# A hybrid-mixer layer on one core: meta tokens in the first attention tile, scans for running sums, per-tile bank drains, an earlier residual fetch and a rearranged end

## The chip, the cores and the metric

One core of one Trainium2 chip runs the whole layer in one launch. The metric is the device time of that launch in microseconds (us); lower is better. TensorE does the products, VectorE (DVE) and ScalarE (ACT) the element-wise work, GpSimd (POOL) a little of it and some transfers, SyncE (SP) issues most transfers.

## The reference, cut to what matters

16 meta tokens stand ahead of 256 tokens of width 2048. The layer is an RMS norm, one wide projection, four mixers of 512 columns each (an SSD state-space mixer, a windowed pooling mixer, FOX attention with a forget bias, and DSA attention whose keys are picked by an index score), an output projection, a residual, and a gated FFN of width 5632 with a short causal convolution on the gate. All in float32; only the last 256 rows are returned.

```python
h = rms_norm(x, g_mix_pre);  u = h @ w_in                      # 272 x 2048 @ 2048 x 4608 (padded)
y_a = ssd(silu(causal_dwconv(xbc)), dt=softplus(..), a=cumsum(dt * -exp(a_log)))
y_b = pool(u_pool);  y_c = fox(q, k, v, cumsum(log_sigmoid(f)));  y_d = dsa(q, c_kv, top 64 keys)
mix = concat(y_a, y_b, y_c, y_d) @ w_out;  x = x + rms_norm(mix, g_mix_post)
h = rms_norm(x, g_ffn_pre)
y = (silu(causal_dwconv(h @ w_gate)) * (h @ w_up)) @ w_down
return (x + rms_norm(y, g_ffn_post))[16:]
```

In FOX the score of a query i and a key j gets the bias F_i - F_j, F being the running sum of log_sigmoid; a softmax over j does not change if F_i is left out.

## The kernel before, in words

Each weight is split into two float32r parts (`split_hi` on ACT, L169, gives `whi`; `split_lo` on DVE, L175, gives `wlo`), and each product is taken three times (L230 to L232: hi*hi, hi*lo, lo*hi). The weights come in tiles of 1 MB, 184 of them in one `queue`; `load` (L134) issues them on SP two tiles ahead into three `raw` buffers, and the parts of the next tile are made while the present one is multiplied.

The projection runs in nine groups of 512 columns (`ORDER`: idx, dq, fk, fq, xs, fv, bc, z, pool), four weight tiles each. A group accumulates four blocks f = 0..3 of 128 columns in four PSUM banks (`acc`, four buffers). In a group's last tile `tile_matmuls` finishes f = 0, 1 in its first half and f = 2, 3 in its second. Then `scale` (L409) multiplies each bank by the row norm on DVE and so drains it; the next group's first product into a bank waits for that.

The mixers are Python generators (`small_values`, `dsa`, `fox`, `ssd`, `pool`). After each half of a weight tile `step(2)` advances the first two of them that are not held back by data, so that their small products lie between the large ones. `drain(name)` runs one to its end when the output projection needs it (order dsa, fox, ssd, pool). Each engine then works in order; its order is chosen by a planner that goes by what should be ready, except for operations under `pin` and in the manual stretch at the start of the FFN.

- `small_values` (L442) makes dt, the decays and their running sums: seven products with a triangular matrix (L485 to L491), transpositions (L500, L501), a row copy `drow` in DRAM, and four selections (L510 to L513).
- `attention` (L550) handles 128 queries at a time (qt = 1, 2): scores (L562, L565), row maximum (L570), eight exponentials (L573), division (L577), a copy of the meta weights (`sm`, L579), transpositions, and one output bank (L601, L606). The two last meta tokens' queries come after that, on their own (L614 to L645).
- `fox` rewrites its biases with sixteen DVE operations (L838, L843). `conv_silu` does the first term of the convolution on DVE (L726), the other three on DVE too (L728), then a Silu on ACT.
- In the first FFN group (two gate tiles, two up tiles, then the other four) `ffn_stats` fetches the tokens as rows into the room of `mo` (L1038, POOL's queue), adds them on DVE (L1047) and makes the second norm.
- The down projection accumulates eight banks (`po`); the last four of its 44 weight tiles are done for token block b = 0 and then for b = 1, each tile through all four banks. Then each block is squared on ACT, weighted on DVE (L1161), normed (L274 to L280) and added to the residual on DVE (L1175), with its transfers alternating between SP and ACT.

Of the kernel before, what the change touches and what calls it, by code (L numbers as in the profile page):

```python
# [1 line left out]

# [19 lines left out]
H = 8  # L22
# [5 lines left out]
OUT_CUTS = ((0, 256), (256, 256), (512, 512), (1024, 512), (1536, 512))  # L28
# [6 lines left out]
FIRST_CUTS = (0, 544, 1072, 1584, 2368, 3152)  # L35
# [19 lines left out]
NCOL = C_OWN + 8  # L55
# [33 lines left out]
def hybrid_layer(ctx: ExitStack, tc, t):  # L89
# [44 lines left out]
    def load(i):  # L134
# [3 lines left out]
        if i:  # L138
            raws[i] = wpool.tile([P, 2048], F32, tag="raw", bufs=3, name="raw")
        else:  # L140
            for q, (c0, c1) in enumerate(zip(FIRST_CUTS, FIRST_CUTS[1:])):
                (nc.scalar if q == 1 else nc.sync).dma_start(packed(c0, c1 - c0), t["first"][:, c0:c1])
            return
# [12 lines left out]
    def split_hi(i, half, n, pool=None):  # L156
# [6 lines left out]
        cuts = [1024 * q // n for q in range(n + 1)] if (i, half) != (0, 0) else [0, 256, 512, 1024]  # L163
# [43 lines left out]
    def tile_matmuls(accs, hi_lo, kts, n, feat, first, last, both=None, skip={}):  # L207
# [45 lines left out]
    def rstd_columns(small, sq, scale, segs, ps, meanwhile=None):  # L253

        n_seg, ng = len(segs), len(sq)
        order = [(g, j, i) for g in range(ng) for j in range(len(sq[g])) for i in (1, 2, 0)]
        for g, j, i in order:
            c0, n = segs[i]
            mm(ps[0:n, g * n_seg + i:g * n_seg + i + 1], sq[g][j][:, c0:c0 + n], ones[:, 0:1],
               start=(g, j, i) == order[0], stop=(j == len(sq[g]) - 1), skip_group_check=True)  # L260
# [24 lines left out]
    def rstd_rows(small, sq, scale, segs, out_rows):  # L285

        y = rstd_columns(small, sq, scale, segs, mix_ps())
        yield
        for g in range(len(sq)):
# [4 lines left out]
            act(out_rows[g], ps2[:, 0:tot], AF.Copy)  # L294

# [43 lines left out]
    G.dma_start(rows, bass.AP(tensor=t["rows"].tensor, offset=t["rows"].offset, ap=[[0, P], [1, 32]]))  # L339
# [53 lines left out]
    def project(g):  # L393
# [6 lines left out]
        for c in range(4):  # L400
            tile_matmuls(accs, lambda k: (xh[:, k, o:L], xl[:, k, o:L]), list(range(4 * c, 4 * c + 4)), n,
                         True, c == 0, c == 3, skip=SKIP.get(g, {}))
            if state["next"] == 4:
                nc.sync.dma_start(cols, t["cols"])
            if state["next"] == 7:
                load_small()
        return accs, n, o

    def scale(g, accs, n, o):  # L409
# [12 lines left out]
        else:  # L422
            u = q4(w=n, name=f"u{g}")
            for f in range(4):
                s = SKIP.get(g, {}).get(f, 0)
                V.tensor_tensor(u[:, f, s:], accs[f][:, s:n], rstd[:, o + s:L], ALU.mult)
                if g == G_Z:
                    act(u[:, f, :], u[:, f, :], AF.Silu)
            U[g] = u
        done.add(g)  # L430

# [10 lines left out]
    def small_values():  # L442
# [41 lines left out]
        pv = ps[:, 0:48].rearrange("p (s c) -> p s c", c=16)  # L484
        mm(pv[0:16, 0, :], upper[0:16, 0:16], val[0:16, 0, :], start=True, stop=True)  # L485
        mm(pv[:, 1, :], ones[0:16, :], val[0:16, 0, :], start=True, stop=False)
        mm(pv[:, 1, :], upper, val[:, 1, :], start=False, stop=True)
        mm(pv[:, 2, :], ones[0:16, :], val[0:16, 0, :], start=True, stop=False)
        mm(pv[:, 2, :], ones, val[:, 1, :], start=False, stop=False)
        mm(pv[:, 2, :], upper, val[:, 2, :], start=False, stop=True)  # L490
        mm(ps[:, 48:56], upper, val[:, 2, 0:8], start=True, stop=True)  # L491
        cum = M.tile([P, 56], F32, tag="cum", name="cum")
        V.memset(cum, 0.0)
        V.tensor_copy(cum[0:16, 0:16], ps[0:16, 0:16])
        V.tensor_copy(cum[:, 16:56], ps[:, 16:56])
        tok["cum"] = cum
        yield
        ps = mix_ps()
        for i, (c0, n) in enumerate(SEG):
            nc.tensor.transpose(ps[0:16, c0:c0 + n], cum[0:n, 16 * i:16 * i + 16], ident[0:n, 0:n])  # L500
        nc.tensor.transpose(ps[0:8, L:L + P], cum[:, 48:56], ident)  # L501
        rsb = M.tile([16, 400], F32, tag="rsb", name="rsb")
        V.memset(rsb, 0.0)
        act(rsb[:, 0:L], ps[0:16, 0:L], AF.Copy)
        act(rsb[0:8, L:400], ps[0:8, L:400], AF.Copy)
        G.dma_start(drow, rsb)
        done.add("rows")
# [3 lines left out]
        mm(ps[:, 16:24], sel_tok, cum[0:16, 0:8], start=True, stop=True)  # L511
        mm(ps[:, 24:32], sel_tok, dtv[0:16, 0, 0:8], start=True, stop=True)
        mm(ps[:, 64:64 + LQ], sel_ssd, rsb[:, L - LQ:L], start=True, stop=True)  # L513
        b0 = M.tile([P, 19], F32, tag="fb0", name="fb0")
        V.tensor_tensor(b0[:, 17:19], ps[:, 14:16], cols[:, C_PARITY:C_PARITY + 2], ALU.mult)
        V.tensor_tensor(b0[:, 16:17], b0[:, 17:18], b0[:, 18:19], ALU.add)
        V.tensor_scalar(b0[:, 0:16], ps[:, 0:16], -1.0, b0[:, 16:17], op0=ALU.mult, op1=ALU.add)
        V.tensor_tensor(b0[:, 15:16], b0[:, 15:16], col(C_MASK15), ALU.add)
# [31 lines left out]
    def attention(name, q, k, v, blk, bias):  # L550

        mh, ml = mixed_out(name)
        for qt, nk in ((1, 144), (2, 272)):
# [3 lines left out]
            for h0 in range(0, H, 2 * nb):  # L557
# [6 lines left out]
                for e, ps in enumerate(pair):  # L564
                    V.scalar_tensor_tensor(s[:, h0 + e:h0 + 2 * nb:2, :],  # L565
                                           ps[:, 0:nb * nk].rearrange("p (a b) -> p a b", b=nk), 0.125,
                                           bias_of(h0 + e, nb), op0=ALU.mult, op1=ALU.add)
# [63 lines left out]
        for _ in range(3):  # L631
            yield
# [613 lines left out]
```

## Time and profile before

| what | value |
|---|---|
| median of 3 runs | 1143.44 us (1143.44 to 1143.46) |
| profiled execution | 1145.26 us, of which the span of the trace is 1143.50 us |
| TensorE busy | 1127.9 us of the span, 7621 instructions |
| VectorE, ScalarE busy | 729.0 us, 556.7 us |
| transfers | 208.31 MB, mean 182 GB/s |
| granted TensorE clock, mean | 0.997 |

The busy time of TensorE counts an instruction until its result is written, and instructions overlap; the time between two starts is what one costs. A wait is put down to the instruction that ended it.

### The profile page before, as it was taken

The numbers are of one execution on the slowest core, as the hardware profiler recorded it, in microseconds if no ns is written. First come the engines' busy times: TensorE is split into PE (matmuls) and PEld (weight loads), VectorE is DVE, ScalarE is ACT, GpSimd is POOL, SyncE is SP. The second block draws the span as 40 slices with busy tenths as digits, with TensorE's granted clock in tenths as the row PEclk, the third lists the DMA queues.
The fourth block names the chain that finished last, engine by engine and source line by source line (L and its number), as shares of the span: only waits on it lengthen the run. The fifth ranks groups of instructions, "written<-read, shape, count | busy, mean of one in ns | idle before, by whom it ended". The sixth has DMA issues, their size and how long they took to land.

```text
span 1143.5 us, 18578 instructions
## 1 busy us (share of the span) xinstructions
PE 1127.9 (99%) x7621; PEld 1028.2 (90%) x7621; DVE 729.0 (64%) x1197; ACT 556.7 (49%) x811; POOL 30.1 (3%) x46
## 2 busy tenths in 40 slices
PE   9999999999999999999999999999999999999996
PEld 9999999988999989999899999998999888888885
DVE  7676595787655978656666576566565644555564
ACT  7334463674444756444544454445444444444452
POOL 0000021000000400000000000000000000000000
PEclk9999999999999999999999999999999999999999
DMA  8644435335455284555555555555555555555552
GB/s 319 246 161 175 150 130 185 130 122 196 157 191 184 88 323 180 177 193 185 184 185 185 185 184 185 184 185 185 184 186 185 191 188 191 193 193 184 184 184 74
DMA packets 32182, 208.31 MB, mean 182 GB/s; under 512 B 3521, under 2 KB 4193, under 8 KB 8801
## 3 DMA queue, kind: packets, MB, share of 16 engines
q1 hardware_dynamic: 29664, 197.49, 48.2%
q0 software_dynamic: 1712, 8.58, 2.3%
q8 instruction: 59, 0.97, 0.3%
q10 hardware_dynamic: 720, 1.06, 0.3%
q14 instruction: 27, 0.21, 0.1%
HBM read 204.99 MB, written 2.12 MB: 181 GB/s over the span
## 4 chain that ended last, share of the span: by engine, by line
PE 92%; DVE 5%; ACT 1%; issue 1%; DMA 1%; SPq 0%; DVEq 0%; ACTq 0%
PE acc L230 14%; PE mx L225 14%; PE acc L232 14%; PE acc L231 14%; PE mx L226 7%; PE acc L1131 4%; PE acc L1133 4%; PE acc L1132 4%; PE mx L1133 4%; PE mx L1131 4%; PE mx L1132 4%; DVE wlo L175 1%; PE mx L230 1%; PE mx L231 1%; PE mx L232 1%
## 5 line engine op out<-in xcount | busy, mean ns | idle before, releaser
L175 DVE TENSOR_TENSOR wlo<-raw,whi 128x1024 fp32r<-128x1024 f32 x369 | 447.8, 1218 | 324.3 <-ACT whi L169 322.7
L169 ACT ACTIVATE whi<-raw 128x1024 fp32r<-128x1024 f32 x369 | 385.0, 1051 | 460.0 <-PE acc L231 194.6
L225 PE MATMUL mx<-hx,whi 128*128 128x512 f32 x704 | 249.0, 396 | 0.0
L232 PE MATMUL acc<-hx,wlo 128*128 128x258 f32 x704 | 198.9, 283 | 1.0 <-DVE wlo L175 1.0
L226 PE MATMUL mx<-hx,wlo 128*128 128x256 f32 x704 | 198.2, 282 | 0.9 <-DVE wlo L175 0.9
L231 PE MATMUL acc<-hx,whi 128*128 128x258 f32 x704 | 198.9, 283 | 0.0
L230 PE MATMUL acc<-hx,whi 128*128 128x258 f32 x704 | 198.3, 283 | 0.0
L225 PEld LDWEIGHTS mx<-hx,whi 128*128 128x128 f32 x704 | 132.6, 188 | 31.1
L230 PE MATMUL acc<-xh,whi 128*128 128x272 f32 (+3 forms) x512 | 151.7, 298 | 1.4 <-DVE st L571 1.0
L231 PE MATMUL acc<-xl,whi 128*128 128x272 f32 (+3 forms) x512 | 146.1, 286 | 0.3 <-DVE xl L353 0.3
L232 PE MATMUL acc<-xh,wlo 128*128 128x272 f32 (+3 forms) x512 | 145.0, 287 | 0.0
L226 PEld LDWEIGHTS mx<-hx,wlo 128*128 128x128 f32 x704 | 133.1, 189 | 1.2 <-DVE wlo L175 1.2
L232 PEld LDWEIGHTS acc<-hx,wlo 128*128 128x128 f32 x704 | 132.9, 189 | 1.2 <-DVE wlo L175 1.2
L231 PEld LDWEIGHTS acc<-hx,whi 128*128 128x128 f32 x704 | 133.4, 189 | 0.3 <-DVE hx L1010 0.2
L230 PEld LDWEIGHTS acc<-hx,whi 128*128 128x128 f32 x704 | 132.4, 189 | 0.6
L230 PEld LDWEIGHTS acc<-xh,whi 128*128 128x128 f32 x512 | 96.5, 189 | 8.2 <-issue 5.2
L231 PEld LDWEIGHTS acc<-xl,whi 128*128 128x128 f32 x512 | 96.7, 189 | 1.3 <-issue 0.7
L232 PEld LDWEIGHTS acc<-xh,wlo 128*128 128x128 f32 x512 | 95.7, 188 | 0.6 <-issue 0.3
L1132 PE MATMUL acc<-whi,yl 128*128 128x512 f32 x176 | 69.6, 395 | 0.0
L1132 PE MATMUL mx<-whi,yl 128*128 128x512 f32 x176 | 69.6, 395 | 0.0
L1133 PE MATMUL mx<-wlo,yh 128*128 128x512 f32 x176 | 69.6, 395 | 0.0
L1133 PE MATMUL acc<-wlo,yh 128*128 128x512 f32 x176 | 69.6, 395 | 0.0
(385 smaller groups left out, 1473.9 us busy)
## 6 DMA issues: line engine op xcount, KB each, us to landing
raw<-w_gate SPq DMA_DIRECT2D x44, 1024.0 KB, 4.8
raw<-w_up SPq DMA_DIRECT2D x44, 1024.0 KB, 4.7
raw<-w_down SPq DMA_DIRECT2D x44, 1024.0 KB, 4.7
raw<-w_in SPq DMA_DIRECT2D x32, 1024.0 KB, 4.8
raw<-w_out SPq DMA_DIRECT2D x16, 1024.0 KB, 4.8
raw<-w_in SPq DMA_DIRECT2D x6, 512.0 KB, 8.7
xT<-xT POOLq DMA_DIRECT2D x1, 2064.0 KB, 12.0
mo<-x_tok POOLq DMA_DIRECT2D x1, 2048.0 KB, 9.9
```

Source lines behind the costliest of these rows:

```text
L169: act(hi[:, c], src, AF.Copy)
L175: V.tensor_tensor(lo, src, hi, ALU.subtract)
L225: mm(accs[f][:, :2 * n], hi[:, c], both(kts[k]), start=st, stop=False)
L226: mm(accs[f][:, n:2 * n], lo[:, c], xh, start=False, stop=en)
L230: mm(out, hi[:, c], xh[:, o:], start=st, stop=False)
L231: mm(out, hi[:, c], xl[:, o:], start=False, stop=False)
L232: mm(out, lo[:, c], xh[:, o:], start=False, stop=en)
L1131: mm(o, yh, hi[:, c], start=(k == 0), stop=False)
L1132: mm(o, yl, hi[:, c], start=False, stop=False)
L1133: mm(o, yh, lo[:, c], start=False, stop=(k == FT - 1))
```

## The change

Nine edits. (1) The first packed transfer is cut at 416 columns, not 544, all five pieces go through SP, and the transfer of `rows` is written behind the first projection group. (2) The running sums are scans along the free dimension on DVE after one transposition; the sums come back by small transpositions, and two selections become one. (3) The two meta queries are scored beside the first attention tile, and their outputs are two more columns of that tile's output products. (4) An attention output is made in two banks of two blocks each. (5) FOX's biases are used as they come, with the opposite sign; the sixteen rewriting operations go. (6) The convolution's first term goes to ACT. (7) From the third group on each bank is scaled right behind its last product. (8) The square sums and row spreads of `rstd_rows` are spread over more steps, and the token rows are fetched into the room of `yT` as soon as the mixers' room is free. (9) In the last four down tiles block 1 goes bank by bank; the norm takes fewer operations, with -0.5 folded into the weights; for block 1 TensorE adds the last 512 columns as a product with a diagonal matrix.

```diff
-FIRST_CUTS = (0, 544, 1072, 1584, 2368, 3152)
+FIRST_CUTS = (0, 416, 1072, 1584, 2368, 3152)
-                (nc.scalar if q == 1 else nc.sync).dma_start(packed(c0, c1 - c0), t["first"][:, c0:c1])
+                nc.sync.dma_start(packed(c0, c1 - c0), t["first"][:, c0:c1])
             if state["next"] == 4:
                 nc.sync.dma_start(cols, t["cols"])
+                G.dma_start(rows, bass.AP(...))            # was issued right behind the first loads
...
                     for k in range(4):
                         pair(f, k // 2, k % 2)
+                    if ended:
+                        ended(f)                            # scale_tile(g, accs, n, o, f)
...
     def rstd_rows(small, sq, scale, segs, out_rows):
-        y = rstd_columns(small, sq, scale, segs, mix_ps())
+        ps = mix_ps()
+        for g in range(len(sq)):
+            square_sums(sq, segs, ps, g)
+            if g < len(sq) - 1:
+                yield
+        y = rstd_columns(small, sq, scale, segs, ps, summed=True)
...
-        mm(pv[0:16, 0, :], upper[0:16, 0:16], val[0:16, 0, :], start=True, stop=True)     # and six more
+        for i, (c0, n) in enumerate(SEG):
+            nc.tensor.transpose(ps[0:16, c0:c0 + n], val[0:n, i, :], ident[0:n, 0:n])
+        V.tensor_tensor_scan(rsb[:, 0:L], one.to_broadcast([16, L]), ps[0:16, 0:L], 0.0, ALU.mult, ALU.add)
+        V.tensor_tensor_scan(rsb[0:8, L:400], one[0:8].to_broadcast([8, P]), ps[0:8, 144:L], 0.0, ALU.mult, ALU.add)
...
+            nc.tensor.transpose(ps[0:n, 16 * i:16 * i + 16], rsb[:, c0:c0 + n], ident[0:16, 0:16])
+        nc.tensor.transpose(ps[:, 48:56], rsb[0:8, L:400], ident[0:8, 0:8])
...
+        def meta_scores():                                  # behind the second pair of score products, qt == 1
+            for pr in range(4):
+                mm(ps[32 * pr:32 * pr + 32, 0:16], qb[:, pr, :], k[:, pr, 0:16], start=True, stop=True)
+            ...                                             # scale, maximum, negate (DVE), Exp (ACT)
+        def meta_weights():                                 # behind the eight exponentials
+            V.reciprocal(s0[:, 19:20], s0[:, 18:19])
+            V.scalar_tensor_tensor(w0..., s0[:, 0:16] repeated, s0[:, 19:20], head mask, op0=ALU.mult, op1=ALU.mult)
+            if m:
+                mm(ps[:, 0:m], w0, cols[:, C_PARITY:C_PARITY + 2], start=True, stop=True)
+            nc.tensor.transpose(ps[:, m:n], sm, ident)
+            for f0 in (0, 2):
+                po = mix_ps()
+                ...                                         # two blocks of n = 130 or 128 columns
+                act(mh[out], pv, AF.Copy)
+                V.tensor_tensor(ml[out], pv, mh[out].bitcast(F32), ALU.subtract)
-        ps = mix_ps()                                       # the meta queries on their own: L614 to L645
-        for _ in range(3):
-            yield
...
-            V.tensor_scalar(out[:, f, o:], u[:, f, o:], col(w + 3), col(C_CONVB + first + f), ...)
+            act(out[:, f, o:], u[:, f, o:], AF.Identity, bias=col(C_CONVB + first + f), scale=col(w + 3))
...
-            pin(V.tensor_scalar(b1[:, h, :], b1[:, h, :], -1.0, cum[:, 24 + h:25 + h], ...))   # x8, and b2 x8
...
+    G.dma_start(bcast(yT, [[D, 2], [1, D]]), t["x_tok"])    # when yT is allocated, ahead of the first FFN group
     def ffn_stats(gate):
-        x2 = bcast(mo, [[D, 2], [1, D]])
-        G.dma_start(x2, t["x_tok"])
-        for _ in range(3):
-            yield
+        x2 = bcast(yT, [[D, 2], [1, D]])
...
+    def down_last():
+        for q in range(4):
+            for k in range(FT - LAST, FT):
+                ...                                         # three products into po[1][q]
+        pin(act(s, st[:, 3:4], AF.Sqrt, bias=mean[3], scale=1.0 / D))
+        V.reciprocal(y, s)
+        V.scalar_tensor_tensor(z, y, mean[4], y, op0=ALU.mult, op1=ALU.mult)
+        V.scalar_tensor_tensor(y, z, 3.0, y, op0=ALU.subtract, op1=ALU.mult)
+        if b:
+            n_v = D - 512
+            ...                                             # ident x xtok into two banks, 6 filler products
+            act(diag, ident, AF.Copy, scale=y)
+            for i, ps in enumerate(sums):
+                mm(ps[:, 0:256], diag, yo[:, c], start=False, stop=True)
+                act(yo[:, c], ps[:, 0:256], AF.Copy)
+                nc.scalar.dma_start(out[:, c], yo[:, c])
+        for c0, n in OUT_CUTS:                              # 512, 512, 256, 256, (512): DVE, then SP
```

## Rows read from the trace of the kernel before

**Rows 1.** Page, busy time: us, share of the span, instructions.

```profile
PE 1127.9 (99%) x7621; PEld 1028.2 (90%) x7621; DVE 729.0 (64%) x1197; ACT 556.7 (49%) x811; POOL 30.1 (3%) x46
```

**Rows 2.** Waits of TensorE, whole run: us in total, times, longest.

```profile
PE acc L232 <- DVE wlo L175: 1.0, 1, 1.0
PE acc L230 <- DVE st L571: 1.0, 1, 1.0
PE mx L583 <- DVE sm L579: 0.9, 2, 0.6
PE mx L776 <- DVE brep L773: 0.6, 1, 0.6
PE acc L231 <- DVE mlpool L896: 0.5, 1, 0.5
```

**Rows 3.** Transfers of 0 to 25 us: GB/s in 40 slices.

```profile
GB/s 0 0 38 104 292 349 407 170 88 162 276 399 409 426 421 405 422 418 394 402 403 387 412 416 423 420 386 417 391 419 388 418 428 433 419 393 347 288 354 393
```

**Rows 4.** Timeline of GpSimd (start, us, engine, line, operation), start and 416 us.

```profile
1.25 0.68 POOL L339 DMA_DIRECT2D rows<-rows  x1 [0.80 <-POOLq L1239]
1.93 0.20 POOL L263 MEMSET rs<- 128x32 f32 x2
...
416.18 0.54 POOL L1117 DMA_DIRECT2D gpost_row<-rows  x1 [18.23 <-DVE sums L1053]
```

**Rows 5.** Timeline of TensorE at 9.9 us.

```profile
9.91 0.40 PE L231 MATMUL acc<-xl,whi 128*128 128x272 f32 x1 [0.34 <-DVE xl L353]
```

**Rows 6.** Timeline of TensorE, running sums of the small values.

```profile
73.03 0.21 PE L485 MATMUL mx<-sp,cst 16*16 16x16 f32 x2
...
74.82 0.37 PE L230 MATMUL acc<-xh,whi 128*128 128x272 f32 x1
```

**Rows 7.** Timeline of TensorE, DSA's meta outputs.

```profile
204.57 0.63 PE L641 MATMUL mx<-p0m,vp 16*64 16x2 f32 x16
```

**Rows 8.** TensorE by stretches: busy (instructions), granted clock, DMA share, GB/s.

```profile
283.10:285.00 1.90, 1.90 (x30) 1.00 1.03 402
286.60:290.10 3.50, 3.50 (x19) 0.51 0.79 247
...
1134.80:1139.80 5.00, 0.00 (x0) 1.00 0.20 68
```

**Rows 9.** Timeline of VectorE around the end of the z projection.

```profile
238.18 0.42 DVE L426 TENSOR_TENSOR uz<-acc,rstd 128x258 f32<-128x258 f32 x1
```

**Rows 10.** Groups of VectorE by shape: busy us, mean ns, idle before.

```profile
L838 DVE TENSOR_SCALAR fb<-fb,cum 128x144 f32<-128x144 f32 x8 | 1.7, 290 | 0.0
L843 DVE TENSOR_SCALAR fb<-fb,cum 128x272 f32<-128x272 f32 x8 | 2.4, 368 | 0.0
L726 DVE TENSOR_SCALAR xs<-uxs,cols 128x272 f32<-128x272 f32 x4 | 1.6, 411 | 0.0
```

**Rows 11.** Groups of ScalarE by shape: busy us, mean ns, idle before.

```profile
L573 ACT ACTIVATE p<-p,st 128x272 f32<-128x272 f32 x8 | 4.1, 510 | 0.0
L1079 ACT ACT_TABLE_LOAD x1 | 1.3, 1283 | 0.0
```

**Rows 12.** Timeline of VectorE in the first FFN group.

```profile
407.25 1.28 DVE L1047 SCALAR_TENSOR_TENSOR xtok<-xtok,rs,mo 128x1024 f32<-128x1024 f32 x1 [2.16 <-DMA mo<-x_tok]
...
413.20 1.22 DVE L175 TENSOR_TENSOR wlo<-raw,whi 128x1024 fp32r<-128x1024 f32 x1
```

**Rows 13.** Transfers of 373 to 420 us: GB/s in 40 slices of 1.175 us.

```profile
GB/s 21 202 418 251 7 0 14 7 0 0 0 0 0 0 0 119 370 390 28 0 0 139 112 432 425 376 432 418 418 425 411 439 397 42 0 0 160 439 377 237
```

**Rows 14.** Timeline of VectorE behind the last product.

```profile
1135.51 0.41 DVE L1169 SCALAR_TENSOR_TENSOR fst<-fst 128x1 f32<-128x1 f32 x2
...
1137.21 2.87 DVE L1175 SCALAR_TENSOR_TENSOR yo<-yo,fst,xtok 128x256 f32<-128x256 f32 x5
```

**Rows 15.** Transfers issued from 1130 us on: KB each, us to landing.

```profile
out_dram<-yo SPq DMA_DIRECT2D x2, 256.0 KB, 2.2
...
out_dram<-yo SPq DMA_DIRECT2D x1, 128.0 KB, 1.9
```

More of the change, by code (lines that the diff above doesn't have):

```diff
@@ L1 @@
 from contextlib import ExitStack
+from functools import partial
 import concourse.bass as bass
@@ L162, in split_hi @@
         steps = []
-        cuts = [1024 * q // n for q in range(n + 1)] if (i, half) != (0, 0) else [0, 256, 512, 1024]
+        cuts = [1024 * q // n for q in range(n + 1)] if (i, half) != (0, 0) else [0, 128, 512, 1024]
         for c in map(slice, cuts, cuts[1:]):
@@ L205, in hybrid_layer, with tile_matmuls @@
     state = {"next": 0}
-    def tile_matmuls(accs, hi_lo, kts, n, feat, first, last, both=None, skip={}):
+    def tile_matmuls(accs, hi_lo, kts, n, feat, first, last, both=None, skip={}, ended=None):
         i = state["next"]
@@ L250, in tile_matmuls, with square_sums, rstd_columns @@
             del halves[i, half]
[L253 to L257, printed above, removed]
+    def square_sums(sq, segs, ps, g):
+        n_seg = len(segs)
+        order = [(j, i) for j in range(len(sq[g])) for i in (1, 2, 0)]
+        for j, i in order:
             c0, n = segs[i]
             mm(ps[0:n, g * n_seg + i:g * n_seg + i + 1], sq[g][j][:, c0:c0 + n], ones[:, 0:1],
-               start=(g, j, i) == order[0], stop=(j == len(sq[g]) - 1), skip_group_check=True)
+               start=g == 0 and (j, i) == order[0], stop=(j == len(sq[g]) - 1), skip_group_check=True)
+    def rstd_columns(small, sq, scale, segs, ps, meanwhile=None, summed=False):
+        n_seg, ng = len(segs), len(sq)
+        if not summed:
+            for g in range(ng):
+                square_sums(sq, segs, ps, g)
         w = ng * n_seg
@@ L498, in small_values @@
         ps = mix_ps()
[L499 to L507, printed above, removed]
-        ps = mix_ps()
         mm(ps[:, 0:16], sel_fox, rsb[:, 0:16], start=True, stop=True)
-        mm(ps[:, 16:24], sel_tok, cum[0:16, 0:8], start=True, stop=True)
-        mm(ps[:, 24:32], sel_tok, dtv[0:16, 0, 0:8], start=True, stop=True)
+        mm(ps[:, 16:32], sel_tok, cum[0:16, 0:16], start=True, stop=True)
         mm(ps[:, 64:64 + LQ], sel_ssd, rsb[:, L - LQ:L], start=True, stop=True)
[L514 to L518, printed above, removed]
+        b0 = M.tile([P, 16], F32, tag="fb0", name="fb0")
+        V.tensor_copy(b0, ps[:, 0:16])
+        V.tensor_tensor(b0[:, 15:16], b0[:, 15:16], col(C_MASK15), ALU.subtract)
         tok["b0"] = b0
@@ L566, in attention @@
                                            ps[:, 0:nb * nk].rearrange("p (a b) -> p a b", b=nk), 0.125,
-                                           bias_of(h0 + e, nb), op0=ALU.mult, op1=ALU.add)
+                                           bias_of(h0 + e, nb), op0=ALU.mult, op1=ALU.subtract)
+                if qt == 1 and h0:
+                    meta_scores()
                 yield
@@ L1150, in hybrid_layer @@
                 down(k, b, ys[k])
+    for k in range(FT - LAST, FT):
+        down(k, 0, ys[k])
+    def down_last():
+        for q in range(4):
+            for k in range(FT - LAST, FT):
+                hi, lo = halves[base + k, q // 2]
+                yh, yl = (a[:, P:2 * P] for a in ys[k])
+                c = slice(512 * (q % 2), 512 * (q % 2) + 512)
+                for y, w in ((yh, hi), (yl, hi), (yh, lo)):
+                    mm(po[1][q], y, w[:, c], start=False, stop=(k == FT - 1 and w is lo))
```

196 lines of the change are left out of this document (100 added, 96 removed).

## The prediction

> **What bounds the kernel now.** I read the page first, then TensorE's waits, then the stretches in which it waits. The reader is to see a kernel that TensorE fills: 1127.9 us of 1143.5 [rows 1]. So an edit pays in three ways only: products that go, waits of TensorE that go, and the stretches at both ends where its work has not begun or is over. The waits are few [rows 2]: 1.0 us for a bank that VectorE had still to drain (put down to `st` L571, the operation beside it), 1.0 us for a `wlo` early in the FFN, 0.9 us for `sm` in two places, 0.6 us for `brep`, 0.5 us for the pool mixer's last output. That is 4.0 us in all: no edit of the middle can pay more than its wait or its products. The profiled execution took 1145.26 us, 1.8 us more than its span of 1143.50, while the median of the runs is 1143.44; the terms below are differences within the span, and I subtract them from the median.
>
> **The change part by part.**
>
> *Start: 0.* Transfers reach 407 GB/s near 4 us, then fall to 170, 88, 162 and 276 for four slices of 0.625 us before they are back at about 410 [rows 3]: (240 + 322 + 248 + 134) x 0.625 = 590 KB missing, 1.4 us late. The small `rows` transfer, issued on GpSimd at 1.25 us [rows 4], is in flight then. TensorE feels it in the third of the first four steps, whose second product starts only at 9.91 us [rows 5]. The edit writes `rows` behind the first group. But nothing on GpSimd's queue makes it wait: the memset of `rs`, written for the second group, ran at 1.93 us, and the transfer of `gpost_row`, written some eight FFN groups later, went out at 416.18 us as soon as its room was free [rows 4]. So I expect `rows` to leave early as before. The lighter first cut may start the first product up to half a microsecond sooner, and the move from ACT's queue to SP's puts one more issue ahead of the later pieces; both are covered by the wait that ends at 9.91. I take 0, bounds +0.3 and -1.2 (the whole 1.4 us less what TensorE must do in any case).
>
> *Running sums: -1.6.* The seven products run from 73.03 to 74.82 us, where the projection resumes [rows 6]: 1.79 us, 0.26 each. They go. Four transpositions become three plus four, with 16 columns at most in the new ones: three more small products, between 0 and 0.26 each; I take 0.1, so +0.3. Four selections become three, -0.26. One more interruption of the stream: +0.15, an estimate. Sum -1.6, bounds -1.1 and -2.1. The scans are not in this trace; they take 400 columns, and even at the slowest per-column rate here, 1.7 us for 8 x 144 columns [rows 10], they are done within 0.6 us, behind half a weight tile of products. If that cover were gone, TensorE would wait those 0.6 us.
>
> *Meta queries: -1.0.* Per attention a run of 16 tiny products of 0.63 us [rows 7], a transposition and one interruption go; one product with two columns comes (0.26 by the figure above), and two columns more on four products. -0.37 without the interruption, -0.67 with 0.3 (an estimate) for it and the transposition; I take -0.5, twice, bounds -0.7 and -1.4. The small DVE work moves beside the first tile, where VectorE otherwise waits for the exponentials. The split output bank adds an eviction per tile, beside projection work: 0, up to +0.2.
>
> *Clock: -1.7.* [...] I take the whole 1.7; the other bound is 0. [...]
>
> *Banks drained tile by tile: -1.0.* The first bank of the z projection is read only at 238.18 [rows 9], behind a row maximum and eight decays on VectorE, when the next group already wants it. Scaled inside its last tile, it is empty half a tile before that, 3.1 us (1127.9 over twice 184 tiles, [rows 1]): the 1.0 us wait goes. What is late next is `brep` and `gm` of the SSD: counting steps, FOX and SSD are one to two half tiles further on, and `brep` then follows the row maximum instead of the division. Its 0.6 us [rows 2] may stay or triple: bounds of this part -1.6 and +1.2.
>
> *DVE relief: -0.6.* The sixteen bias operations are 1.7 + 2.4 us, the first convolution terms 0.41 us each, eight of them [rows 10]. They lie between the DSA scores and `sm`, so of the two waits for `sm` (0.9 us) I take 0.6 away; bounds 0 and -0.9. The moved terms stand in ScalarE's queue, where a run of eight exponentials is 4.1 us and a table load 1.28 [rows 11]. [...]
>
> *Pool mixer: -0.5.* Its last parts were forced out in a row when the projection wanted them; with FOX done four steps earlier it gets those steps in time. -0.5 [rows 2], bounds 0 and -0.7.
>
> *FFN residual: -1.0.* VectorE stood 2.16 us until the token rows landed, and its four adds pushed a `wlo` to 413.20 [rows 12], for which TensorE waited 1.0 us [rows 2]. The transfer was in flight with three weight tiles. The room of `yT` is free when the output projection ends, near 377 us, and from 378 to 390 us almost nothing is transferred [rows 13]. On GpSimd's queue the transfer goes ahead of the residual adds; its issue takes about as long as the two in [rows 4]. So the whole 1.0; bounds -1.1 and 0. The scaling of `gpost_row` by -0.5 is one DVE pass of 2048 columns, two microseconds or less, beside products: 0.
>
> *End: -1.2.* VectorE's last adds are 2.87 us from 1137.21 [rows 14], and a 256 KB transfer lands 2.2 us later [rows 15]. Bank by bank, three of four banks are squared and weighted before the last product, and one small operation of about 0.2 us goes from the norm: y is ready 0.2 to 0.3 sooner. Three quarters of the adds remain on VectorE: -0.7. The last piece is 128 KB, 1.9 us: -0.3. Sum -1.2. The diagonal product must keep up: from y a scaling, two products, two evictions and two issues, by my estimate 2.1 us until the last is issued, as long as the adds that remain; TensorE's clock stays at 1.00 for 5 us after the last product [rows 8]. Bounds -0.7 and -1.5.
>
> Sum: 0 - 1.6 - 1.0 - 1.7 - 1.0 - 0.6 - 0.5 - 1.0 - 1.2 = -8.6, so 1143.44 - 8.6 = 1134.8 us.
>
> **The rivals.**
>
> *The slow clock stays or moves: 1136.5.* The 1.7 us are not gained. [...] Against it: no stretch as thin as the one before 286.6 is left. With a second slow stretch 1138.2.
>
> *VectorE takes it back: 1139.0.* Products that go from the middle only bring TensorE sooner to the same DVE results. Then running sums, meta queries, drains and relief give nothing: 1134.8 + 1.6 + 1.0 + 1.0 + 0.6 = 1139.0. For it: after the change score maximum, decays and `brep` meet within two half tiles. Against it: VectorE is busy 64% and loses some 7 us.
>
> *The start does gain: 1133.8.* `rows` leaves late after all, the third step's data come 1.4 us sooner, and 1.0 of it reaches TensorE. Against it: rows 4.
>
> *Slower: 1153.2.* VectorE's convolution waits in order for ScalarE's Identity. Where that stands behind eight exponentials and a table load it is 4.1 + 1.3 = 5.4 us late [rows 11]; behind it on VectorE wait `wlo` parts, and half a tile of 3.1 us is the cover: 2.3 us on TensorE, eight times 18.4 us. Slower than before by over 0.2% it is from five of eight on: 8.6 + 2.3 = 10.9, over 2.3. Against it: the planner puts first what is ready, and the eight terms are spread over two places.
>
> **How the numbers follow.** Forecast 0.54, slow clock 0.17, VectorE 0.14, start 0.10, slower 0.05. All lower bounds together are -12.1, about 1131.3, and I end the range at 1131.2; upward it takes in the slow clock and VectorE's case with half a microsecond more, 1139.5. What is outside is half of VectorE's case, the slower one and a little below, under 0.2. 0.2% is 2.3 us, about what a measurement of this kernel can tell from no change. Faster (below 1141.2): 0.54 + 0.17 + 0.10 and 0.06 of VectorE's 0.14, so 0.87. The other 0.08 of it I give to no change, and 0.05 to slower.
>
> **What would show it.** The first product of the third step still near 9.9 us and `rows` among GpSimd's first instructions (start). No run of products at 0.5 clock before the end (clock). No wait of TensorE for a z bank, for `mlpool` or for a `wlo` near 413 us; the token rows landed before 390 us. The last product over at 1127.4 us instead of 1134.8, and 7.5 us instead of 8.7 from there to the end of the span. Wrong I am if the waits for `brep`, `sm` or a convolution term add up to more than 2 us, or if VectorE's row of the middle shows idle time that ends on ScalarE's Identity.

## The result, and the profile after

The changed kernel takes 1134.59 us in the median of four executions (1132.21 to 1135.87), the kernel before 1143.45 beside it: a ratio of 0.992, 95% interval 0.9902 to 0.9937. The forecast of 1134.8 us is met to 0.2 us, and by accident: a gain of 6.6 us for which it has no term covers four terms that failed. The profiled execution took 1134.62 us, 1.7 us more than its span of 1132.9.

The same large product, counted off in both traces, shows where the time went (us, changed kernel less kernel before; one profiled execution each):

| up to the product at | difference there | this stretch | forecast for it |
|---|---|---|---|
| 13 us, behind the first four steps | +1.1 | start +1.1 | 0 |
| 89 us | -0.1 | running sums -1.2 | -1.6 |
| 306 us | -3.75 | middle -3.7 (meta queries, banks, DVE relief, pool) | -3.1 |
| 437 us | -3.80 | FFN residual 0 | -1.0 |
| last down product, 1123 us | -10.36 | down projection -6.6 | no term |
| end of the span | -10.6 | end -0.25 | -1.2 |

The clock is not in this table, since both profiled executions have a slow stretch, some 3.4 us in which TensorE's granted clock is about 0.50; it costs 3.41 x 0.50 = 1.7 us, an estimate from the changed kernel's stretch (shown below). The medians don't compare like that. The kernel before took 1143.44 us where, by its time, it had no such stretch; its profiled execution, with it, took 1145.26. The changed kernel's profiled execution, one of the two that make its median, has one. So by medians the clock cost +1.7 where -1.7 was forecast, and 1.1 - 1.2 - 3.7 + 1.7 - 0.05 - 6.6 - 0.25 = -9.0 is the -8.9 measured. That is luck too: beside the later runs the kernel before had medians of 1143.96, 1145.41 and 1145.07 us, 1143.6 to 1144.0 at a mean clock of 0.998 and 1144.7 to 1146.1 below it. Of the times given further down, one execution of b_gap (1211.63 us at a mean clock of 0.849) and one of a_rep (1822.83 us at 0.556) are left out.

TensorE on the page of the changed kernel, against [rows 1] (busy us, share, instructions):

```profile
PE 1120.3 (99%) x7598; PEld 1027.2 (91%) x7598; DVE 722.6 (64%) x1173; ACT 556.3 (49%) x817; POOL 32.5 (3%) x46
```

Its waits (total, times, longest) answer to [rows 2]; one of 1.1 us at the very start, in both kernels, is not shown. The waits for z's bank, `brep`, `sm`, the pool mixer and the `wlo` of 413 us are gone from the list; new are a long one at the start (`whi` L172), one for a copy on GpSimd, two for `hx` and one at the end (`diag`):

```profile
PE acc L233 <- ACT whi L172: 2.0, 1, 2.0
PE mx L874 <- POOL repfox L563: 1.9, 1, 1.9
PE mx L229 <- DVE wlo L178: 1.3, 1, 1.3
PE acc L234 <- DVE hx L1032: 0.6, 2, 0.4
PE acc L1222 <- ACT diag L1219: 0.4, 1, 0.4
```

The `wlo` wait of 1.3 us, at 396 us, was there before with 0.9; [rows 2] leaves that one out:

```profile
PE mx L226 <- DVE wlo L175: 0.9, 1, 0.9
```

TensorE by stretches (busy and instructions of PE, PEld, DVE, ACT, POOL; granted clock; DMA share; GB/s), changed kernel; the first two are its long waits, the third its slow stretch, the counterpart of 286.60 to 290.10 in [rows 8]:

```profile
6.68:8.93 2.25, 0.29 (x4) 0.07 (x2) 0.03 (x1) 0.63 (x1) 0.00 (x0) 1.00 1.02 409
175.57:177.77 2.20, 0.29 (x4) 0.06 (x2) 2.19 (x4) 0.53 (x2) 2.14 (x1) 1.00 0.91 384
179.01:182.42 3.41, 3.41 (x18) 3.41 (x17) 0.00 (x0) 0.92 (x1) 0.00 (x0) 0.50 0.71 283
900.00:1000.00 100.00, 100.00 (x443) 82.84 (x442) 51.53 (x56) 45.48 (x57) 0.00 (x0) 1.00 0.55 197
```

The last row is the find. The same 100 us of the kernel before:

```profile
900.00:1000.00 100.00, 100.00 (x430) 80.53 (x429) 49.44 (x55) 43.20 (x54) 0.00 (x0) 1.00 0.52 186
```

Both run without a wait at a granted clock of 1.00, with the same products, and yet 443 fit in where 430 did: 226.7 ns from start to start instead of 233.3. A busy share of 100% hides it; the count shows it.

### The profile page after: what moved, and what is told of

Same layout as the page of the kernel before. It is cut to its first block, busy times and chain, and to the rows that moved or that the text cites. A ratio compares the mean times of both kernels' runs of the same rounds, so it can differ in the third digit from the quotient of the medians.

```text
span 1132.9 us, 18508 instructions
## 1 busy us (share of the span) xinstructions
PE 1120.3 (99%) x7598; PEld 1027.2 (91%) x7598; DVE 722.6 (64%) x1173; ACT 556.3 (49%) x817; POOL 32.5 (3%) x46
## 4 chain that ended last, share of the span: by engine, by line
PE 96%; DVE 2%; DMA 1%; issue 0%; POOL 0%; ACT 0%; SPq 0%; ACTq 0%; DVEq 0%; POOLq 0%
PE acc L233 16%; PE acc L235 15%; PE acc L234 15%; PE mx L228 14%; PE mx L229 7%; PE acc L1155 4%; PE acc L1154 4%; PE acc L1153 4%; PE mx L1155 3%; PE mx L1154 3%; PE mx L1153 3%; PE mx L1184 1%; PE mx L610 1%; PE mx L233 1%; PE mx L234 1%; DVE wlo L178 1%
## 5 line engine op out<-in xcount | busy, mean ns | idle before, releaser
L172 ACT ACTIVATE whi<-raw 128x1024 fp32r<-128x1024 f32 x369 | 385.0, 1051 | 467.2 <-PE acc L234 205.5
L1153 PE MATMUL acc<-whi,yh 128*128 128x512 f32 x176 | 68.5, 389 | 0.0
L1154 PE MATMUL mx<-whi,yl 128*128 128x512 f32 x160 | 62.2, 389 | 0.0
```

Of the source, the lines that this page charges most:

```text
L172: act(hi[:, c], src, AF.Copy)
L1153: mm(o, yh, hi[:, c], start=(k == 0), stop=False)
L1154: mm(o, yl, hi[:, c], start=False, stop=False)
```

## Experiments

The kernel before, run beside these, took 1143.6 to 1146.1 us, so each result has its ratio to it.

### Why is the down projection quicker? Addresses

A product has a stationary operand, that of its LDWEIGHTS row (442 such rows stand beside the 443 products above), and a moving one. The constants grew by 8 columns, so everything allocated behind them moved by 32 bytes. Within 256 bytes the moving operands `whi`, `wlo` (512 columns) now begin at 224, where the stationary `yh`, `yl`, placed from the other end of the memory, always began; before they began at 192. Three kernels test that.

**b_gap**, the shift alone:

```diff
     cols = const.tile([P, NCOL], F32, name="cols")
+    const.tile([P, 8], F32, name="gap")
```

> The kernel before with one edit: 32 unused bytes per partition behind the constants, so that everything allocated after them lies 32 bytes further on, as in the changed kernel, whose constants are 32 bytes longer. The tiles at the other end of the memory (yh, yl of the down projection) stay where they are. Address theory: the products of the down projection took 233.3 ns from start to start before and 226.7 ns after the change, with the same instructions, because their moving operand (whi, wlo) came to lie at the same offset within 512 bytes as their stationary one (yh, yl): 480 and 480 instead of 448 and 480. Then this kernel has 226.7 ns over the 40 tiles of 24 products and 1143.4 - 960 x 6.67 ns = 1137.0 us, all else as before. Rival, program theory: the rate comes from something else in the changed program (the order of its last products, its instruction stream, what VectorE and ScalarE do meanwhile): 233.3 ns and 1143.4 us here.

Measured 1137.9 us, ratio 0.9946 (0.9929 to 0.9962): 1136.88 and 1137.13 us at a mean clock of 0.998, 1138.64 and 1138.97 at 0.997. Against 1143.6 to 1144.0 of before at 0.998 that is -6.8 us: 32 unused bytes give what the address theory says, 6.4. The time per product was not read here.

**a_shift**, all edits without the shift (256 bytes instead of 32):

```diff
+    const.tile([P, 56], F32, name="gap")
```

> The changed kernel with 224 unused bytes per partition behind the constants: its lower allocations then lie 256 bytes further on than those of the kernel before, not 32, and the operands of the down projection stand to each other as before (moving at 192, stationary at 224 within 256 bytes). All edits are in. Address theory: 233.3 ns per product of the down projection again, 960 x 6.67 ns = 6.4 us back, 1134.6 + 6.4 = 1141.0 us: the change without the shift is worth some 2.5 us. Rival, the edits do it: 226.7 ns stay and the time is 1134.6.

Measured 1140.46 us, ratio 0.9952 (0.9934 to 0.997), and the old count, 430 or 431 products in 100 us:

```profile
900.00:1000.00 100.00, 100.00 (x431) 80.51 (x430) 50.16 (x54) 43.76 (x54) 0.00 (x0) 1.00 0.53 189
```

By medians the shift is worth 5.9 us, by the spans of the profiled executions 6.8. The nine edits by themselves are worth 3.0 us against the 1143.45 beside the result and 5.0 against the 1145.41 beside a_shift; between the two profiled executions, with one slow stretch each, they are worth 3.9 (1143.5 to 1139.6).

**b_map**, the distance varied by tile:

```diff
-        yh = Y.tile([P, SEQ], F32R, tag="yh", bufs=LAST + 1, name="yh")
+        yh = Y.tile([P, 512], F32R, tag="yh", bufs=LAST + 1, name="yh")[:, off:off + SEQ]   # yl too
```

> The kernel before, yh and yl of the down projection each inside a tile of 2048 bytes per partition, at an offset that changes with the tile k of the weights: 32 k bytes for k 0 to 15, 448 + 8 (k - 16) for 16 to 31, 468 + 4 (k - 32) for 32 to 39. So the distance d from the stationary to the moving operand's first byte, taken modulo 512, goes through 480 - 32 k, then 32, 24, 16, 8, 0, 504 ... 424, then 12, 8, 4, 0, 508 ... 496. Relative theory: what counts is d, and d = 0 is quick (226.7 ns), d = 480 and d = 384 are slow (233.3): then k = 15, 20 and 35 are quick though both operands begin at 448 (a multiple of 64) and not at 480. Rival, absolute parity: quick is what begins at an odd multiple of 32 in both operands: no tile quick here, because the moving one stays at 448. Rival, relative with a short period: quick at every d that is a multiple of 64 (or of 256). The table of rate against d is the result; the time is 1143.4 less 24 x 6.67 ns = 0.16 us per quick tile, 1142 to 1143 us.

Measured 1143.60 us in the one execution, where 1142 to 1143 was expected. The distance is counted from the stationary to the moving operand. Six tiles (24 products each) by their stretches, at distances 256, 224, 32, 0, 32 and 0 in this order; the quick ones take 5.45 us, the others 5.59:

```profile
927.20:932.65 5.45, 5.45 (x26) 4.51 (x24) 2.76 (x4) 2.44 (x4) 0.00 (x0) 1.00 0.51 185
932.65:938.24 5.59, 5.59 (x25) 4.51 (x24) 2.82 (x4) 2.42 (x4) 0.00 (x0) 1.00 0.55 196
966.16:971.75 5.59, 5.59 (x25) 4.51 (x24) 2.81 (x4) 2.42 (x4) 0.00 (x0) 1.00 0.52 188
971.75:977.20 5.45, 5.45 (x25) 4.51 (x24) 2.76 (x4) 2.44 (x4) 0.00 (x0) 1.00 0.53 185
977.20:982.80 5.60, 5.60 (x25) 4.51 (x24) 2.83 (x4) 2.42 (x4) 0.00 (x0) 1.00 0.58 202
999.43:1004.89 5.46, 5.46 (x26) 4.51 (x24) 2.74 (x4) 2.42 (x4) 0.00 (x0) 1.00 0.54 177
```

Over all 40 tiles the mean from start to start is 226.8 to 227.9 ns at distances 0, 256 and 4, 228.3 at 16, 229.4 at 64 and 320, and 229.7 to 233.7 at all others, 233.4 at 128 and 192. In the first 16 tiles, in steps of 32 bytes, distances that differ by 256 agree within 0.1 ns. So, with b_gap, it is the distance that counts, with a period of 256 bytes. Between those steps the pattern is irregular: 12 bytes is slow, 16 is not. The parity theory is out: both operands at a multiple of 64 were slow at distance 448 and quick at 0.

So the place of the two operands decides between 226.7 and 233.3 ns a product. Why is open.

**a_hx**, the same in the first two FFN projections:

```diff
-    hx = HP.tile([P, 2, KT, LQ], F32R, name="hx")
+    hx = HP.tile([P, 2, KT, 320], F32R, name="hx")[:, :, :, 38:38 + LQ]
```

> The changed kernel with the rows of hx (the moving operand of the FFN's first two projections) 1280 bytes long instead of 1032 and begun so that the 512-column products have both their blocks of 256 columns at the offset of the stationary operand within 256 bytes (224). Nothing else changes. In the changed kernel these 704 products take 233.2 ns on average from start to start, spread from 229 to 238 by tile. If the rule found in the down projection (quick where the distance is a multiple of 256 bytes) holds for any products of 512 columns: 226.7 ns, 704 x 6.5 ns = 4.6 us less, 1130.0 us. Rival, it holds for products of one block of 512 columns alone: no gain, 1134.6. The products of 258 and 256 columns (120 and 119 ns) have not shown any dependence of this size; should the new distance of -8 bytes cost them 2 ns each, 4.2 us of it would be lost again.

Measured 1128.01 us, ratio 0.9853 (0.9838 to 0.9867), 6.6 us below the changed kernel; 6.2 of it build up evenly over the FFN. Groups of TensorE's products from 440 to 880 us (busy, mean ns of one), first the changed kernel, then a_hx:

```profile
L228 PE MATMUL mx<-hx,whi 128*128 128x512 f32 x628 | 221.8, 396 | 0.0
L229 PE MATMUL mx<-hx,wlo 128*128 128x256 f32 x627 | 176.4, 281 | 0.0
L233 PE MATMUL acc<-hx,whi 128*128 128x258 f32 x607 | 171.8, 283 | 0.0
```

```profile
L228 PE MATMUL mx<-hx,whi 128*128 128x512 f32 x640 | 222.4, 392 | 0.0
L229 PE MATMUL mx<-hx,wlo 128*128 128x256 f32 x640 | 178.2, 278 | 0.0
L233 PE MATMUL acc<-hx,whi 128*128 128x258 f32 x604 | 170.0, 281 | 0.0
```

The theory's direction is right and its shares are wrong: from start to start in this window the 512-column products gain 3.0 ns, not 6.5 (their moving operand has two blocks), but the 256-column ones gain 2.8 and those of 258 columns 1.2, where none or a loss was expected. The 256-column ones read `hx` from the same place as the 512-column ones (`hh[:, k, 2:LQ]`), so they came to distance 0 too; the -8 of the expectation is that of the 258-column ones alone. What the two blocks still cost is open.

### The start

**a_twoq**, the second piece on ScalarE's queue again:

```diff
-                nc.sync.dma_start(packed(c0, c1 - c0), t["first"][:, c0:c1])
+                (nc.scalar if q == 1 else nc.sync).dma_start(packed(c0, c1 - c0), t["first"][:, c0:c1])
```

> The changed kernel with one part undone: the second piece of the first transfer goes on ScalarE's queue again, not as the second of five on SyncE's. Queue theory: the changed kernel's later pieces land at 8.22, 9.27 and 10.26 us instead of 5.30, 8.06 and 9.06 because each is issued one place later; with two queues again the third piece lands near 5.3, the second step begins near 7.0 us instead of 8.93, and the projection from the third step on is 1.05 us earlier: 1 us less than the changed kernel. Rival, hole theory: the slow stretch of the transfers (92 to 160 GB/s for some 2.5 us) starts when the packets of the small rows transfer get their turn, and falls ahead of the third piece whichever queue carries the second: third piece again at about 8 us, gain under 0.4 us.

Measured 1132.64 us, ratio 0.9897 (0.9877 to 0.9916). The third piece lands at 5.12 us instead of 8.22, and the second step follows on the first without a break; the steady projection is 1.3 us ahead of the changed kernel, where 1 was expected. TensorE there (start, duration), first the changed kernel, then a_twoq:

```profile
6.68 0.29 PE L235 MATMUL acc<-xh,wlo 128*128 128x272 f32 x1
8.93 0.39 PE L233 MATMUL acc<-xh,whi 128*128 128x272 f32 x1 [1.96 <-ACT whi L172]
```

```profile
7.17 0.29 PE L235 MATMUL acc<-xh,wlo 128*128 128x272 f32 x1
7.29 0.29 PE L233 MATMUL acc<-xh,whi 128*128 128x272 f32 x1
9.74 0.40 PE L234 MATMUL acc<-xl,whi 128*128 128x272 f32 x1 [0.33 <-DVE xl L371]
```

The queue theory holds; its rival doesn't. The cause is surer than the size. In all six profiled executions with the changed kernel's start the third piece lands between 7.34 and 8.71 us and TensorE waits 1.6 to 2.3 us; but a_hx, one of them, is itself 1.0 us ahead of the changed kernel at 60 us. So the +1.1 of the table is one execution's.

**a_late**, `rows` truly late:

```diff
-                G.dma_start(rows, bass.AP(...))
+                nc.sync.dma_start(rows, bass.AP(...))      # behind cols
```

> The changed kernel with the rows transfer on SyncE's queue behind that of cols, so that it cannot leave before some 23 us; it left at 1.25 us on GpSimd's. Theory: its slow packets make the hole in the first transfers (92 to 160 GB/s between about 3.4 and 5.6 us); without them there is no hole, the third piece lands near 6.3 us instead of 8.22, the second step begins near 7.2 us instead of 8.93 and the projection is 1.5 us earlier from there on. Rival: the hole is one of the first transfers themselves (first use of the queues, fetch of descriptors or of instructions) and stays: third piece near 8.2 us, no gain.

Measured 1131.05 us, ratio 0.9879 (0.9859 to 0.9899). Transfers of 0 to 25 us (GB/s in 40 slices), changed kernel, then a_late:

```profile
GB/s 0 0 37 235 283 292 116 105 246 295 362 396 420 430 408 393 430 414 383 412 403 390 402 420 429 413 385 393 423 428 385 403 439 426 426 393 157 105 144 131
```

```profile
GB/s 0 0 29 212 301 369 316 324 325 349 344 294 282 261 276 322 392 427 403 415 417 408 430 424 400 419 402 414 394 383 408 418 433 426 419 406 223 184 249 419
```

The hole (116 and 105) is filled: 16 KB issued on GpSimd held up the first pieces. The third lands at 6.28 us, the projection is 1.1 us ahead of the changed kernel (1.5 expected). Against the kernel before it gains nothing that lasts: 0.8 us ahead at 9.2 us, 0.2 at 13.8, level at 60. Another 2.7 us came unasked: the wait for `repfox` fell to 0.8 us, and the slow stretch behind it did not come.

### The wait for repfox, and the clock

In the changed kernel the copies run on GpSimd while VectorE splits weights (start, duration), GpSimd and then VectorE:

```profile
174.39 0.29 POOL L563 COPY repfox<-ufv 128x128 f32<-128x128 f32 x1 [0.71 <-DVE ufv L451]
175.33 2.38 POOL L563 COPY repfox<-ufv 128x128 f32<-128x128 f32 x1 [0.65 <-DVE ufv L451]
```

```profile
174.85 0.42 DVE L451 TENSOR_TENSOR ufv<-acc,rstd 128x272 f32<-128x272 f32 x1
175.19 2.34 DVE L178 TENSOR_TENSOR wlo<-raw,whi 128x1024 fp32r<-128x1024 f32 x2
```

One copy is 0.29 us, the next, beside two splits, 2.38, as long as they last. The copy before these two, at 172.31 beside one split of 1.21 us, took 1.22.

**a_rep**:

```diff
         done.add("v_fox")
+        yield
         blk = block_diagonal("fox")
```

> The changed kernel with one more step between GpSimd's copies repfox and the transpositions that read them, so that these come half a weight tile (about 3 us) later. In the changed kernel TensorE waits 2.07 us for the last copy, which took 2.38 us beside VectorE's work, and 1.2 us after the wait its granted clock is 0.5 for 3.41 us, 1.7 us lost. Chain theory: the wait went in with the drains tile by tile, which let the copies' readers be issued in the half tile in which the last tile is scaled; and the wait brings the slow stretch. Then both go: 2.07 + 1.7 = 3.8 us less than the changed kernel's profiled run, about 1129 us of span. Rival, free-running clock: only the wait goes, the slow stretch stays or moves elsewhere, 2.1 us less (span near 1130.8). Rival, the wait moves to a later reader of the same chain: no gain.

Measured 1130.99 us, ratio 0.9883 (0.9867 to 0.99); span of the profiled execution 1130.3. The wait is gone; 0.4 us come back at 243.6. No slow stretch at 179; this time there was one at 9.13 to 12.54, right behind the long wait of the start (8.73). That is the rival's outcome for this execution; two others took 1130.36 and 1130.99 us at a mean clock of 0.999, so by their times without it.

The other profiled executions agree: where TensorE waits 1.6 to 2.3 us at the start, at 177 us or at both, one slow stretch of 3.41 us stands behind one such wait (changed kernel, a_twoq and a_hx from 177 to 179 us on; a_shift, a_stats and a_onlyz from 9.4 to 10.7 on); in a_late, whose waits there are 0.4 and 0.8 us, there is none before the end, nor in best, whose longest is 1.6 us at 416 us. That the waits bring the stretch is likely and not shown: no run put a wait in. A long wait is not the only way to one: the kernel before and b_map, without a wait over 1.3 us, have theirs behind thin products at 285 to 287 us. The changed kernel's four executions have mean clocks of 0.999, 0.998, 0.997 and 0.996, and their times stand in that order but for 0.07 us: the spread of 3.7 us goes with the clock. How many stretches each caught was not seen, save in the profiled one.

**a_onlyz**, drains tile by tile for z alone:

```diff
-        group = project(g, None if late else lambda accs, n, o, f: scale_tile(g, accs, n, o, f))
+        group = project(g, lambda accs, n, o, f: scale_tile(g, accs, n, o, f) if g == G_Z else None)
...
+        if g != G_Z:
+            scale(g, *group)
```

> The changed kernel with the drains tile by tile kept for the z projection alone; every other projection is scaled behind its group, as before the change. Chain theory: in the changed kernel the drain by tile makes the value group of FOX ready inside its last half tile, so that the transpositions of repfox are issued there and TensorE waits 2.07 us for GpSimd's last copy; scaled behind the group they come later and that wait goes, while z's bank is still empty in time (no wait of 0.9 us for it): 2.1 us less than the changed kernel, and no slow clock behind 179 us. Rival, the copies themselves are slow (4.3 us in all instead of 2.0) wherever they stand: a wait for repfox of over 1 us stays. Rival, the second half of the edit: with the others scaled behind the group a wait for a bank shows elsewhere.

Measured 1134.63 us, ratio 0.9908 (0.989 to 0.9926): nothing gained. The wait for `repfox` and the stretch at 179 are gone, as the chain theory says, and z's bank is not waited for; but the slow stretch came at 9.4 us instead, and so did another wait of the same length (waits of TensorE):

```profile
PE acc L233 <- ACT whi L172: 2.3, 1, 2.3
PE mx L639 <- DVE sm L630: 2.1, 1, 2.1
```

It stands at 244 us behind FOX's second set of exponentials. So the chain theory is right on the wait, not on the gain, and the third theory's wait is not for a bank. My reading, from this one wait, is that with products out of the middle TensorE meets the mixers' chain a little further on.

### The FFN residual

The token rows land at 381.61 us, early as forecast. VectorE in the changed kernel (start, duration): the first addition goes among the operations that make `hx`:

```profile
382.62 0.41 DVE L1027 TENSOR_TENSOR mo<-mo,mx 128x258 f32<-128x258 f32 x1
382.95 1.43 DVE L1066 SCALAR_TENSOR_TENSOR xtok<-xtok,rs,yT 128x1024 f32<-128x1024 f32 x1
384.30 0.96 DVE L1032 SCALAR_TENSOR_TENSOR hx<-xT,cols,hx 128x258 fp32r<-128x258 f32 x1
```

**a_stats**:

```diff
-                V.scalar_tensor_tensor(dst, dst, y[:, i + 1:i + 2], x2[:, i, c], ...)
+                pin(V.scalar_tensor_tensor(dst, dst, y[:, i + 1:i + 2], x2[:, i, c], ...))
```

> The changed kernel with the four operations that add the token rows held in the written order, behind the preparation of hx. In the changed kernel the rows land at 381.61 us, so the planner puts the first addition (1.43 us on VectorE, at 382.95) among the operations that make hx, and TensorE waits 0.24 and 0.38 us for hx and 1.31 us for a wlo (0.88 before). Theory: that is where the gain of the FFN edit went; behind hx the waits for hx go and that for wlo is 0.9 us again, 1.1 to 1.4 us less. Rival: VectorE is late there in any case, the waits only move behind: within 0.3 us of the changed kernel.

Measured 1133.66 us, ratio 0.9902 (0.9882 to 0.9922). The waits for `hx` are gone, that for `wlo` is shorter, and the second norm is now late:

```profile
PE mx L229 <- DVE wlo L178: 1.0, 1, 1.0
PE acc L294 <- DVE rs L291: 0.8, 1, 0.8
```

At 437 us it is 0.7 us ahead of the changed kernel: half of what was expected.

### The version that the runs point to

**best** joins a_late, a_rep, a_hx and a_stats, and adds:

```diff
             diag = E.tile([P, P], F32, name="diag")
+            E.tile([P, 32], F32, name="gap")               # last weight tiles to distance 0
-OUT_CUTS = ((0, 512), (512, 512), (1024, 256), (1280, 256), (1536, 512))
+OUT_CUTS = ((0, 256), (256, 256), (512, 512), (1024, 512), (1536, 512))
```

> The changed kernel with what the runs so far point to: rows behind cols on SyncE's queue (1.1 us at the start), one step more ahead of repfox's readers (2.1 us, and with neither long wait left no slow clock stretch before the end, 1.7 us), rows of hx of 1280 bytes at the stationary operand's offset (6.2 us in the FFN's first two projections), the additions of the token rows held behind hx (0.5 us), the two last weight tiles of the down projection moved by 128 bytes to their stationary operand's offset (48 products x 6 ns, 0.3 us), and the first 512 output columns in two pieces, so that the first transfer leaves 0.27 us sooner (0.25 us if the 1 MB of output limits the end, which runs at some 350 GB/s from 1 us behind the first issue; nothing if the last additions do). From the changed kernel's profiled 1134.6 us: 1134.6 - 1.1 - 2.1 - 1.7 - 6.2 - 0.5 - 0.3 - 0.25 = 1122.5 us, and a spread of the runs under 0.5 us instead of 3.7, as no wait long enough for a slow stretch is left. Rival: the parts overlap (the later repfox and the earlier start meet VectorE at other places) and new waits take up to 2 us back: 1124.5. Rival for the clock: slow stretches come anyway, 1124.2 in some runs and a spread of 2 us or more.

Measured 1123.04 us, ratio 0.981 (0.9796 to 0.9823): quicker than both kernels. Four executions lie within 0.44 us (1122.83 to 1123.27); a fifth, 1124.90 at a clock of 0.997, by its time caught a slow stretch after all. Expected were 1122.5 and no slow stretch. Its waits:

```profile
PE acc L294 <- DVE rs L291: 1.6, 1, 1.6
PE mx L229 <- DVE wlo L178: 1.1, 1, 1.1
PE acc L233 <- ACT whi L172: 0.5, 2, 0.3
```

What is left is in the first FFN group: holding back the additions costs here nearly as much as it saves. The last weight tiles gave the 0.3 us expected. The finer output pieces gave nothing: the first transfer leaves 0.26 us sooner behind the last product, the last lands 0.1 us later.

## Why the prediction was right, and where it was wrong

- *The step that is missing.* The eight columns added to the constants were not costed at all. They are the change's largest effect, -6.6 us, shown by b_gap, a_shift and b_map. "TensorE is filled" was read as "only products and waits can go"; the time per product was taken as given.
- *Start: 0.* Wrong step: the further issue ahead of the later pieces was taken as "covered by the wait that ends at 9.91". `rows` did leave at 1.25 us, as forecast, but with one queue for five pieces the second step waits 2 us and that cover is gone: +1.1 in the table's pair (a_twoq). The rival that the start gains 1.0 us is not borne out even once `rows` really is late: a_late's steady projection is level with that of the kernel before.
- *Clock: -1.7.* The term is the stretch of [rows 8], 3.50 us at a granted clock of 0.51: an estimate of 3.50 x 0.49 = 1.7 us. This stretch, behind 30 tiny products in 1.90 us, went; two long waits came and a stretch behind one of them, 3.41 us at 0.50. The first rival named that. And the term was taken off a median whose executions did not have the stretch: the 1.8 us between profiled execution and median, set down in the prediction, was the clock, as the later times of that kernel show. What decides where a stretch comes was not shown: with the same two waits, the changed kernel and a_hx have it behind the second, a_shift and a_stats behind the first.
- *Banks: -1.0.* z's bank and `brep` came out well; what was late next was neither, but `repfox` (1.9 us), which stood in no bound. Without it an `sm` wait of 2.1 us (a_onlyz).
- *Running sums, meta queries, DVE relief, pool.* Sums -1.2 for -1.6. The others can't be told apart by the runs; with the bank term -3.7 for -3.1, and -5.6 if the `repfox` wait is taken out, among them `sm` down from 0.9 us to nearly nothing and the pool wait gone. No wait for a convolution term showed: the slower rival is out.
- *FFN residual: -1.0.* The wait near 413 went, the rows landed before 390, both as forecast. The failing step is "So the whole 1.0": nothing was set against the additions in their new place, and they went where VectorE had no room (a_stats), +0.6 for `hx` and +0.4 for a `wlo`. The list of waits that the prediction adds up to 4.0 us lacks that `wlo`, at 0.9.
- *End: -1.2.* From the last product to VectorE's last addition it is 1.0 us shorter, as worked out, against [rows 14]; to the end of the span only 0.2. The last product was over at 1124.4 us, not 1127.4, and 8.5 us follow it, not 7.5. The 128 KB pieces take 2.5 to 2.7 us, not the 1.9 of [rows 15] (KB each, us to landing):

```profile
out_dram<-yo SPq DMA_DIRECT2D x2, 256.0 KB, 2.1
out_dram<-yo ACTq DMA_DIRECT2D x2, 128.0 KB, 2.5
out_dram<-yo SPq DMA_DIRECT2D x2, 128.0 KB, 2.7
```

The transfers of the end, in 40 slices (GB/s), the kernel before from 1137 to 1143.5 us, then the changed one from 1126.5 to 1132.9:

```profile
GB/s 50 0 0 0 0 0 0 0 0 95 321 315 271 359 240 13 315 365 403 391 303 403 391 353 391 391 403 391 303 38 0 0 0 0 0 0 0 0 0 0
```

```profile
GB/s 0 0 0 0 0 0 0 0 0 0 243 384 358 371 359 410 410 358 359 320 314 365 352 320 359 346 307 371 243 7 0 0 0 0 0 0 0 0 0 0
```

The 1 MB now goes out without a gap at some 350 GB/s; if that rate sets the end, earlier additions can't bring it forward. But best, whose first transfer left 0.26 us sooner, should then have ended sooner, and it did not: that is the outcome which its expectation gave to the last additions as the limit, and its smaller first pieces left gaps, down to 51 GB/s. So the 128 KB pieces' longer way is shown, what limits the end is open.

- *The sums.* The lower bounds of the parts add up to -12.2 us, not -12.1; nothing hangs on it. No run shows the 0.15 and 0.3 us set down for an interruption of the stream; what was measured is -1.2 for the running sums with it in.

## What to carry to other kernels

Where TensorE never waits, look at the time from one product to the next, and at where its two operands begin: a quiet shift of 32 bytes outweighed nine edits here (5.9 us against 3.0 to 5.0 by medians). A forecast for an edit has to follow its allocations, and the data that it makes ready earlier, since a planner will put work there whether or not that engine has room. Before a stretch is taken off a median, see whether the median's executions have it.

## What the runs showed of the hardware

- Products of 512 columns with a 128x128 stationary operand took 226.7 ns from start to start in the changed kernel's down projection, where the moving and the stationary operand begin at the same place within 256 bytes, and 233.3 in the kernel before, where they begin 32 bytes apart. b_map has other distances: 226.8 to 227.9 ns at 0, 256 and 4, 228.3 at 16, 229.4 to 233.7 elsewhere; a_hx has the smaller effect on 256 and 258 columns, 2.8 and 1.2 ns.
- A 16 KB transfer on GpSimd's queue beside the first loads took their rate from some 320 GB/s (a_late) to 105 and 116 (changed kernel) for over a microsecond; on SyncE's queue, behind them, it did not.
- A GpSimd copy of 0.29 us took 1.22 us beside one `wlo` split on VectorE and 2.38 beside two (changed kernel, 172 to 178 us).
- TensorE's granted clock fell to 0.50 for 3.41 us within 1.4 us behind a wait of some 2 us, in some executions behind the one such wait, in others behind the other; in the kernel before it fell to 0.51 over 3.50 us behind thin products, without such a wait.
